# Six durations in a host-side scheduler of a decoder block set to the traced ones

## The chip, the cores and the metric

The kernel runs on one core of one Trainium2 chip. The metric is the device time of one launch in microseconds (us). The time before is the median of three runs.

The engines are named as the profile names them: PE (TensorE, with PEld for its weight loads), DVE (VectorE), ACT (ScalarE), POOL (GpSimd) and SP (the queue that issues the DMAs).

## What is computed

One decoder layer over 1024 tokens of width 1024: a normalisation modulated by a condition c, one wide projection, sparse attention and a Mamba-2 scan side by side, a gated merge, and a feed-forward part. Cut to what matters:

```python
h = rms_norm(x, norm1_w[l]) * (1.0 + sc1) + sh1
proj = h @ w_in[l]
q, kv, nsa_g, z, xbc, dt_raw, mg = jnp.split(proj, IN_OFFSETS, axis=-1)
...
o_attn = nsa_attention(q, kc, kv[:, :, 1], ks, kv[:, :, 3], kw, kv[:, :, 5], nsa_gates,
                       cmp_pe_k[l], cmp_w1_k[l], cmp_w2_k[l], cmp_pe_v[l], cmp_w1_v[l], cmp_w2_v[l])
...
xbc = jax.nn.silu(xbc)
...
y = ssd_chunked(xs, dt, a, bm, cm) + d_skip.astype(jnp.float32)[:, None] * xs.astype(jnp.float32)
y = y.reshape(b, s, SSM_INNER) * jax.nn.silu(z.astype(jnp.float32))
```

## The kernel before

**Tiling.** Every large product is float32, split into a high and a low part: `mm3k` (L319 to L324) issues three matmuls per k-tile, high times high, low times high and high times low (L322, L323, L324). Weights are loaded raw, ACT makes the high part `whi` (L351) and Pool the low part `wlo` (L353).

**Stages, in order of time.** The start (normalisation, `token_block` for keys, values and queries, up to about 250 us); the attention (two groups of heads g, eight query tiles i and two halves hq, units named g_i_hq), with the projections of x, z and m in its background; the scan (four groups g, eight chunks c, named g_c), with what is left of the background; the output projections and the second normalisation; the gated products (`gate_up`), from about 1860 us; `down` and the end.

**What sets the order.** A scheduler written in the host program, class `Flow`, decides in which order the instructions of each engine are written; the chip then runs each engine's queue in just that order. A stage is a set of generators that yield requests for PE: `yield (needs, cost, trace)`. `cost` is a number in us, and PE's own clock of the scheduler is advanced by it. Work of ACT, DVE, POOL and the DMAs is put into four queues with costs of its own, times `RESERVE` (1.15, 1.15, 1.2 and 1.0). The scheduler's clock picks what is ready first.

In the attention the background is a fill. It may go while its credit is above zero. The credit falls by the cost of each background request and grows by the cost of each main request times a fixed pace:

```python
            if s is fill:
                self.credit -= cost
            elif pace is not None:
                self.credit = min(self.credit + cost * pace(), 20.0)
```

**Names around the change.** In `background` (L1154 to L1281) blocks of kind x, z and m take turns. A block has four parts q, each with eight requests, accumulated into `fps`. For x, parts 0 and 2 are the first halves of the tokens; `finish_x` evacuates `fps` to `xr`, clears its first three columns on POOL (memset, L1173) if it is a first half, else copies them from the half before (L1179); then DVE makes three convolution steps into `u` (L1166), ACT a tanh, DVE a last step (L1184), and PE transposes u to `xsT` (L1199), which is stored to `xsd`.

A modulation row is made on POOL in `mod_rows` (L1377 to L1394): four loads of `w_ada`, each scaled (L1389), and eight sums into `acc` (L1392).

In the attention, `tp` is the transposed probability P (L2353), `kv` the copy of it in float32 halves (ACT L2356 the high one, DVE L2357 the low one), and `o` takes the value products (L1100). POOL scales P (L2287). `kv0` and `kv1` are also the tiles of keys and values of the two groups, loaded at L1057. DVE's and ACT's writes go to the two spare parts of the same tile.

In the scan, per chunk: `cb` (L2434), `bdm` (DVE L2436), the decay `E` (eight DVE instructions, L2422), the diagonal product `yd` (L2454) that reads `xs` (loaded at L2401), `yo` (L2463) and `sp` (L2485).

## Time and profile before

| | us |
|---|---|
| median of three runs | 2515.34 (2510.87 to 2517.52) |
| the profiled execution, its time | 2509.3 |
| its span | 2507.5 |
| PE busy | 2433.3 |
| DVE busy | 1784.3 |
| ACT busy | 1240.3 |
| POOL busy | 1163.9 |

The span runs from the first to the last instruction of the profiled execution; 1.8 us of its time lie around it. A wait is the idle time of an engine ahead of an instruction, put down to what released it last. The chain of work that ended last is for 81% PE.

### The profile page before, as it was taken

How to read it: one execution, taken by the hardware profiler on the slowest of the kernel's cores; microseconds unless marked ns; L12 is line 12 of the kernel's file. 1: busy time of each engine (PE TensorE's matmuls, PEld its weight loads, DVE VectorE, ACT ScalarE, POOL GpSimd, SP SyncE). 2: the span in 40 equal slices, each digit the busy share in tenths (PEclk: the TensorE clock that was granted, in tenths of full speed). 3: DMA queues.
4: the chain of work that ended last, by engine and by line, in shares of the span. 5: the costliest groups of instructions: out<-in, count | busy, mean ns of one | idle time of the engine just before them, and what ended most of it. 6: DMA issues, size and time to landing. Idle time of an engine off the chain costs nothing.

```text
span 2507.5 us, 39721 instructions
## 1 busy us (share of the span) xinstructions
PE 2433.3 (97%) x13674; PEld 2081.8 (83%) x13674; DVE 1784.3 (71%) x3917; ACT 1240.3 (49%) x2644; POOL 1163.9 (46%) x917
## 2 busy tenths in 40 slices
PE   5999999999999999999999999999999999999998
PEld 5999788899888988988777777878988888887886
DVE  7644788867766788776567886778767676765858
ACT  4422677666655676656456555532443323323543
POOL 2112474656464747455534342201245565655853
PEclk8999999999999999999999999999999999999999
DMA  7432443333335433235467876426343332326853
GB/s 252 132 126 83 158 120 96 89 102 110 93 102 167 141 97 114 81 104 187 145 192 233 266 228 193 147 76 225 137 173 101 105 106 93 113 92 233 308 169 118
DMA packets 274474, 363.91 MB, mean 145 GB/s; under 512 B 22232, under 2 KB 177624, under 8 KB 273760
## 3 DMA queue, kind: packets, MB, share of 16 engines
q1 hardware_dynamic: 274272, 361.37, 44.8%
q8 instruction: 108, 1.77, 0.3%
q14 instruction: 94, 0.77, 0.1%
HBM read 256.05 MB, written 105.25 MB: 144 GB/s over the span
## 4 chain that ended last, share of the span: by engine, by line
PE 81%; DVE 9%; DMA 4%; ACT 3%; issue 2%; POOL 1%; SPq 0%; DVEq 0%; ACTq 0%; POOLq 0%
PE fps L322 7%; PE fps L324 6%; PE fps L323 6%; PE gu L323 6%; PE gu L322 6%; PE gu L324 6%; PE o L1100 4%; PE S L2269 4%; PE tp L2353 4%; PE dps L324 2%; PE dps L323 2%; PE dps L322 2%; PE sps L322 2%; PE tokps L324 2%; PE tokps L322 2%; PE tokps L323 2%
## 5 line engine op out<-in xcount | busy, mean ns | idle before, releaser
L2287 POOL TENSOR_SCALAR P<-P,sm,gate 128x640 f32<-128x640 f32 (+7 forms) x256 | 228.0, 901 | 275.2 <-DVE sm L2284 176.1
L2357 DVE TENSOR_TENSOR kv<-tp,kv 128x512 fp32r<-128x512 f32 (+1 forms) x296 | 191.9, 657 | 103.1 <-ACT kv L2356 101.8
L2356 ACT ACTIVATE kv<-tp 128x512 fp32r<-128x512 f32 (+1 forms) x296 | 167.1, 574 | 183.7 <-PE tp L2353 174.9
L2278 ACT ACTIVATE P<-P,sm 128x640 f32<-128x640 f32 (+7 forms) x256 | 187.2, 733 | 50.4 <-DVE sm L2274 48.2
L1100 PE MATMUL o<-kv 128*128 128x512 f32 x528 | 189.2, 407 | 6.1 <-DVE kv L2357 3.5
L2269 PE MATMUL S<-kv,Q 128*128 128x384 f32 (+5 forms) x768 | 183.6, 336 | 5.1 <-DVE sm L2274 4.3
L322 PE MATMUL fps<-hT_hi,whi_x 128*128 128x512 f32 x384 | 160.4, 418 | 0.7 <-ACT xs L1209 0.7
L2274 DVE CUSTOM_DVE_ANT_0 P<-S,kb 128x256 f32<-128x256 f32 (+5 forms) x256 | 121.3, 493 | 49.2 <-PE tp L2353 31.9
L2353 PE MATMUL tp<-id,P 128*128 128x128 f32 x1056 | 155.2, 273 | 0.0
L324 PE MATMUL fps<-hT_hi,wlo_x 128*128 128x512 f32 x384 | 151.2, 394 | 0.0
L323 PE MATMUL fps<-hT_lo,whi_x 128*128 128x512 f32 x384 | 150.9, 393 | 0.0
L322 PE MATMUL fps<-whi_z,hT_hi 128*128 128x256 f32 x512 | 150.4, 294 | 0.0
L2269 PEld LDWEIGHTS S<-kv,Q 128*128 128x128 f32 x768 | 128.1, 189 | 25.5 <-DVE sm L2274 8.5
L1923 DVE TENSOR_TENSOR ex<-ex,gu 128x512 f32<-128x512 f32 x120 | 80.9, 684 | 94.5 <-PE gu L324 93.8
L1166 DVE SCALAR_TENSOR_TENSOR u<-xr,hcw,u 128x512 f32<-128x512 f32 x144 | 138.9, 967 | 10.9 <-ACT u L1169 7.3
L2353 PEld LDWEIGHTS tp<-id,P 128*128 128x128 f32 x1056 | 128.2, 140 | 22.1 <-issue 0.2
L324 PE MATMUL fps<-whi_z,hT_lo 128*128 128x256 f32 x512 | 144.8, 283 | 0.0
L323 PE MATMUL fps<-wlo_z,hT_hi 128*128 128x256 f32 x512 | 144.6, 282 | 0.0
L1758 ACT ACTIVATE x1r<-ex 128x512 fp32r<-128x512 f32 x102 | 62.9, 627 | 121.1 <-POOL ex L1776 60.4
L1100 PEld LDWEIGHTS o<-kv 128*128 128x128 f32 x528 | 96.0, 189 | 24.9 <-DVE kv L2357 8.0
L2427 POOL TENSOR_TENSOR dx<-xs,hd 128x512 f32<-128x512 f32 x32 | 41.8, 1308 | 160.0 <-DVE yy L2469 123.4
L322 PE MATMUL fps<-hT_hi,whi_m 128*128 128x512 f32 x256 | 113.7, 444 | 0.0
(480 smaller groups left out, 8042.1 us busy)
## 6 DMA issues: line engine op xcount, KB each, us to landing
wada<-w_ada SPq DMA_DIRECT2D x40, 512.0 KB, 4.3
actd<-ex SPq DMA_DIRECT2D x69, 256.0 KB, 2.0
ex<-actd SPq DMA_DIRECT2D x69, 256.0 KB, 4.0
ac<-acd SPq DMA_DIRECT2D x32, 512.0 KB, 4.7
raw_x<-w_in SPq DMA_DIRECT2D x24, 512.0 KB, 4.6
ws<-w_down SPq DMA_DIRECT2D x44, 256.0 KB, 3.6
wsd<-ws SPq DMA_DIRECT2D x88, 128.0 KB, 1.8
ff<-w_gate SPq DMA_DIRECT2D x22, 512.0 KB, 4.9
```

Source lines behind the costliest of these rows:

```text
L322: mm(ps, lh, rh, start=k == 0, stop=False)
L323: mm(ps, lh, rl, start=False, stop=False)
L324: mm(ps, ll, rh, start=False, stop=k == kt - 1)
L1100: nc.tensor.matmul(o.t.rearrange("p h q -> p (h q)"), vst(), pair()[m], start=n + m == 0, stop=n == u.total - 1 and m == 1)
L1166: return lambda: nc.vector.scalar_tensor_tensor(u.t, xr[:, k:k + N2], hcw[:, ft, k:k + 1], u.t, op0=OP.mult, op1=OP.add)
L2269: mm(sp[:, :w], q, kvb.kv[:, br, r, first + c0:first + c1], start=r == 0, stop=r == 1)
L2274: nc.vector.tensor_tensor_reduce(P[:, c0:c1], sp[:, :w], k.kb[:, m0:m0 + w], scale=-1.0, scalar=sm[:, 0, h:h + 1] if p else 3.0e38, op0=OP ...
L2278: ex = A(0.26 + 0.8333e-3 * n, [mx], lambda: nc.scalar.activation(P[:, :n], P[:, :n], AF.Exp, bias=sm[:, 1, h:h + 1], scale=-1.0, accum_ou ...
L2287: nc.gpsimd.tensor_scalar(P[:, :n], P[:, :n], sm[:, 3, m:m + 1], k.gate[:, i, self.h0 + m, br + 1:br + 2], op0=OP.mult, op1=OP.mult)
L2353: nc.tensor.transpose(tp[:, h * 128:h * 128 + 128], P, k.id)
L2356: hi = A(0.064 + 0.104 * n, [op, pair], lambda: nc.scalar.activation(pair()[0][:, c], tp[:, c], AF.Copy))
L2357: lo = V(0.068 + 0.133 * n, [hi], lambda: nc.vector.tensor_sub(pair()[1][:, c], tp[:, c], pair()[0][:, c]))
```

## The change

Six cost numbers of requests are other ones: of the token products (`tokps`), of the background products (0.72 for z, 0.69 for x and m, where both had 0.685), of the output projection (`ops`), of the sums of `turn_x` on POOL, of the gated products (`gu`) and of the down products (`dps`). No instruction is added or taken away.

```diff
--- before.py
+++ after.py
@@ -658,7 +658,7 @@
                 for k in range(8):
                     while self.hop[t0 // 2][k // 2] is None:
                         yield None
-                    op = yield ([W.ops[k], ps, self.hop[t0 // 2][k // 2]], 0.356, lambda t=t, k=k, s=s, ps=ps: self.mm3k(
+                    op = yield ([W.ops[k], ps, self.hop[t0 // 2][k // 2]], 0.363, lambda t=t, k=k, s=s, ps=ps: self.mm3k(
                         ps[:, t], k, 8, self.hT_hi[:, k, s], self.hT_lo[:, k, s], W.hi[:, k], W.lo[:, k]))
             if kd == "kv":
                 self.kv_evac(b, t0, ps, op)
@@ -1261,7 +1261,7 @@
                             c, s = slice(m * 128, (m + 1) * 128), slice(h * N2, (h + 1) * N2)
                             self.mm3k(ps.t, k, 8, W.hi[:, k, c], W.lo[:, k, c], self.hT_hi[:, k, s], self.hT_lo[:, k, s])
                         need = W.ops[k]
-                    op = yield ([need, ps], 0.685, mm)
+                    op = yield ([need, ps], 0.72 if kd == "z" else 0.69, mm)
                     if n > len(self.order) - 3 and k == 3:
                         while self.o[0] is None:
                             yield None
@@ -1617,7 +1617,7 @@
             ps = self.buf("s", [128, 256], "ops")
             for k in range(8):
                 m = lambda r, k=k: r[:, 2 * (t % 2) + k // 4, k % 4, 64 * (t - t % 2):64 * (t - t % 2) + 128]
-                op = yield ([W.ops[k], self.mop[t // 4][k], ps], 0.356, lambda: self.mm3k(
+                op = yield ([W.ops[k], self.mop[t // 4][k], ps], 0.359, lambda: self.mm3k(
                     ps.t, k, 8, m(self.M0), m(self.M1), W.hi[:, k], W.lo[:, k]))
             left[n] -= 1
             if left[n] == 0:
@@ -1702,7 +1702,7 @@
 
             def add(E, need, o, x, y, op=OP.subtract, cost=None):
                 eng = nc.vector if E is V else nc.gpsimd
-                return E(cost or (0.6 if E is V else 1.23), need, lambda: eng.tensor_tensor(o(), x(), y(), op=op), first=True)
+                return E(cost or (0.6 if E is V else 1.45), need, lambda: eng.tensor_tensor(o(), x(), y(), op=op), first=True)
 
             def copy(need, o, x, cost=0.52):
                 return A(cost, need, lambda: nc.scalar.activation(o(), x(), AF.Copy), first=True)
@@ -1904,7 +1904,7 @@
                     (hi, lo), (rh, rl) = (r[:, 128 * k:128 * k + 128] for r in pc.t), moving[p](k)
                     self.mm3k(ps.t, k, 4, hi, lo, rh, rl)
 
-                op = yield ([w, ps] + need, 0.685, product)
+                op = yield ([w, ps] + need, 0.697, product)
             pc.until(op)
             self.ff_sums(s, p, q, b, ps, op)
         self.ffend = op
@@ -2139,7 +2139,7 @@
                         outs.clear()
                 (xp, xe), (wp, we) = self.dl[p, b]
                 ps, js = banks[j], slice(128 * j, 128 * j + 128)
-                op = yield ([xe, we, ps], 0.685, lambda: self.mm3k(
+                op = yield ([xe, we, ps], 0.69, lambda: self.mm3k(
                     ps.t, b, NB, xp.t[0][:, js], xp.t[1][:, js], wp.t[0], wp.t[1]))
                 if j == 3:
                     xp.until(op)
```

Of PE's 11,800 rows the order is the same in the gated and down stages. From the attention's first unit to the scan's last group it is another one; a few rows of the start move too. Numbers at the ends of names are those of tiles; they differ between the programs.

**POOL, where group 0 of the attention ends and block x7 runs in the background.** `acc31` is a modulation row, `wlo_z4` the low part of the next block's weights, `xr` the tile whose head is cleared. Before, the row of the clearing for part 0 of x7 stands behind the first sum:

```order
L1389 TENSOR_TENSOR wada312_8136<-wada312_8136,sc_75 128x1024
L1392 TENSOR_TENSOR acc31_8171<-acc31_8171,wada310_8134 128x512
L1173 MEMSET xr_8223 128x3
L1392 TENSOR_TENSOR acc31_8171<-acc31_8171,wada310_8134 128x512
L1392 TENSOR_TENSOR acc31_8171<-acc31_8171,wada312_8136 128x512 x2
L1389 TENSOR_TENSOR wada314_8278<-wada314_8278,sc_75 128x1024
L2287 TENSOR_SCALAR P0_7_1_8194<-P0_7_1_8194,sm0_7_1_8067,gate_1659 128x640
```

After, it stands behind the last sum and the first half of wlo_z4:

```order
L1392 TENSOR_TENSOR acc31_8193<-acc31_8193,wada316_8298 128x512
L2287 TENSOR_SCALAR P0_7_1_8226<-P0_7_1_8226,sm0_7_1_8021,gate_1659 128x640
L1392 TENSOR_TENSOR acc31_8193<-acc31_8193,wada316_8298 128x512
L353 TENSOR_TENSOR wlo_z4_8426<-raw_z4_0_8375,whi_z4_8411 128x1024
L1173 MEMSET xr_8310 128x3
L353 TENSOR_TENSOR wlo_z4_8426<-raw_z4_4_8429,whi_z4_8411 128x1024
L1140 TENSOR_TENSOR ws51_8452<-ws51_8452 128x256 x3
L1173 MEMSET xr_8506 128x3
```

The second clearing (xr_8506), of part 2, which before stood ahead of the second half of wlo_z4, is now behind it and three rows of `ws51` (a repeated row is printed once, with its count).

**DVE, at the same place.** Before, the convolution of part 0 (u_8246 from xr_8223) runs between the exponentials of the last unit:

```order
L1166 SCALAR_TENSOR_TENSOR u_8246<-xr_8223,hcw_76,u_8246 128x512
L1113 TENSOR_TENSOR ot0_7_0_8269<-o0_7_0_7806,ob0_7_0_8253 64x256
L1114 TENSOR_TENSOR ot0_7_0_8269<-o0_7_0_7806,ob0_7_0_8253 64x256
L1166 SCALAR_TENSOR_TENSOR u_8246<-xr_8223,hcw_76,u_8246 128x512
L2274 ISA P0_7_1_8244,sm0_7_1_8067<-S0_7_1_8250,kb_85,sm0_7_1_8067 128x384
```

After, it is the u_8317 from xr_8310, with three of the unit's steps for `kv0` behind its first row:

```order
L2357 TENSOR_TENSOR kv0_2840<-tp0_7_1_8415,kv0_2840 128x512
L2357 TENSOR_TENSOR kv0_2840<-tp0_7_1_8421,kv0_2840 128x512
L1184 SCALAR_TENSOR_TENSOR u_8389<-xr_8385,u_8389 128x512
L1166 SCALAR_TENSOR_TENSOR u_8317<-xr_8310,hcw_76,u_8317 128x512
L2357 TENSOR_TENSOR kv0_2840<-tp0_7_1_8446,kv0_2840 128x512
L1166 SCALAR_TENSOR_TENSOR u_8317<-xr_8310,hcw_76,u_8317 128x512
L2357 TENSOR_TENSOR kv0_2840<-tp0_7_1_8460,kv0_2840 128x512
L1166 SCALAR_TENSOR_TENSOR u_8317<-xr_8310,hcw_76,u_8317 128x512
L2357 TENSOR_TENSOR kv0_2840<-tp0_7_1_8475,kv0_2840 128x512
L1184 SCALAR_TENSOR_TENSOR u_8317<-xr_8310,u_8317 128x512
```

The kv0 rows are those that the last value products of group 0 read; they were ahead of or between other blocks' steps, and three of them now come behind a step that reads what POOL has cleared.

**PE, at the start of the scan.** `yd0_0` to `yd0_5` are the diagonal products of chunks 0 to 5 of group 0. Before, those of chunks 0 and 1 have only sp and cb between them, and the load of xs for chunk 2 follows the use of its buffer by chunk 0:

```order
L323 MATMUL fps_14205<-hT_lo_214,whi_m4_13998 128x512
L324 MATMUL fps_14205<-hT_hi_210,wlo_m4_14002 128x512
L2454 MATMUL yd0_0_14245<-xs0_0_14129,E0_0_14153 128x64 x8
L2485 MATMUL sp0_0_14254<-xw0_0_14137,bdm0_0_14131 128x512
L2434 MATMUL cb0_2_14256<-bct0_2_14180 128x128
L2454 MATMUL yd0_1_14271<-xs0_1_14141,E0_1_14184 128x64 x8
L322 MATMUL fps_14205<-hT_hi_210,whi_m4_13998 128x512
```

After, yd0_1 is followed by its yo, and 78 background matmuls stand between yd0_1 and yd0_2 (24 before):

```order
L323 MATMUL fps_14145<-hT_lo_214,whi_m4_14036 128x512
L324 MATMUL fps_14145<-hT_hi_210,wlo_m4_14043 128x512
L2434 MATMUL cb0_2_14214<-bct0_2_14181 128x128
L2454 MATMUL yd0_1_14216<-xs0_1_14102,E0_1_14126 128x64 x8
L2463 MATMUL yo0_1_14227<-st0_0_14186,bct0_1_14098 128x512
L322 MATMUL fps_14145<-hT_hi_210,whi_m4_14036 128x512
L323 MATMUL fps_14145<-hT_lo_214,whi_m4_14036 128x512
```

Chunks 3 to 5 stand closer after. Before, yd0_3 had 27 background matmuls up to yd0_4:

```order
L322 MATMUL fps_14494<-hT_hi_210,whi_m5_14035 128x512
L323 MATMUL fps_14494<-hT_lo_214,whi_m5_14035 128x512
L324 MATMUL fps_14494<-hT_hi_210,wlo_m5_14046 128x512
L2454 MATMUL yd0_3_14500<-xs0_3_14348,E0_3_14371 128x64 x8
L322 MATMUL fps_14494<-hT_hi_210,whi_m5_14035 128x512
L323 MATMUL fps_14494<-hT_lo_214,whi_m5_14035 128x512
```

After, yo and sp follow yd0_3 at once, and 12 matmuls, of which the first two rows are shown, lead to yd0_4 (and again 12 from there to yd0_5):

```order
L323 MATMUL fps_14487<-hT_lo_214,whi_m5_14176 128x512
L324 MATMUL fps_14487<-hT_hi_210,wlo_m5_14190 128x512
L2434 MATMUL cb0_4_14508<-bct0_4_14462 128x128
L2454 MATMUL yd0_3_14510<-xs0_3_14377,E0_3_14350 128x64 x8
L2463 MATMUL yo0_3_14533<-st0_2_14478,bct0_3_14233 128x512
L2485 MATMUL sp0_3_14537<-xw0_3_14442,bdm0_3_14359 128x512
L322 MATMUL fps_14487<-hT_hi_210,whi_m5_14176 128x512
L323 MATMUL fps_14487<-hT_lo_214,whi_m5_14176 128x512
```

## Rows read from the trace of the kernel before

**Rows 1.** The page: busy time of PE, share of the span, instructions.

```profile
PE 2433.3 (97%) x13674; PEld 2081.8 (83%) x13674; DVE 1784.3 (71%) x3917; ACT 1240.3 (49%) x2644; POOL 1163.9 (46%) x917
```

**Rows 2.** Windows: busy us (instructions) of PE, PEld, DVE, ACT, POOL; PEclk; DMA; GB/s.

```profile
750.00:800.00 50.00, 46.57 (x331) 43.23 (x330) 27.22 (x81) 24.89 (x76) 22.58 (x28) 0.97 0.59 187
1250.00:1300.00 50.00, 47.77 (x229) 37.74 (x229) 27.08 (x67) 28.83 (x66) 19.45 (x13) 0.97 0.60 186
713.80:745.10 31.30, 31.30 (x171) 26.44 (x170) 22.27 (x48) 18.97 (x41) 25.41 (x18) 1.00 0.35 100
754.70:758.10 3.40, 3.40 (x17) 3.10 (x16) 3.08 (x4) 1.76 (x3) 2.08 (x1) 0.50 0.58 177
1302.00:1312.00 10.00, 10.00 (x52) 7.86 (x50) 9.20 (x26) 6.25 (x16) 3.68 (x4) 1.00 0.58 190
```

**Rows 3.** Waits of PE, whole span: total us, times, longest us.

```profile
PE h2T L1668 <- ACT x L1649: 3.7, 3, 2.7
PE xsT L1199 <- DVE u L1184: 2.1, 2, 1.8
PE gu L323 <- DVE M L1705: 1.9, 1, 1.9
PE yd L2454 <- DMA xs<-xsd: 1.7, 1, 1.7
PE fps L324 <- POOL wlo_m L353: 1.7, 1, 1.7
PE kT L746 <- DVE kk L714: 1.6, 1, 1.6
PE hidmm L960 <- DMA w1whi<-cmp_w_k: 0.9, 1, 0.9
```

**Rows 4.** Timeline of POOL near x7: start, us, line, operation, count, idle before.

```profile
713.80 3.76 POOL L1389 TENSOR_TENSOR wada<-wada,sc 128x1024 f32<-128x1024 f32 x2
717.50 1.29 POOL L1392 TENSOR_TENSOR acc<-acc,wada 128x512 f32<-128x512 f32 x1
718.73 0.10 POOL L1173 MEMSET xr<- 128x3 f32 x1
728.56 0.88 POOL L2287 TENSOR_SCALAR P<-P,sm,gate 128x640 f32<-128x640 f32 x1 [2.49 <-DVE sm L2284]
734.67 1.64 POOL L2287 TENSOR_SCALAR P<-P,sm,gate 128x640 f32<-128x640 f32 x1
736.27 1.73 POOL L1392 TENSOR_TENSOR acc<-acc,wada 128x512 f32<-128x512 f32 x1
742.73 2.41 POOL L353 TENSOR_TENSOR wlo_z<-raw_z,whi_z 128x1024 fp32r<-128x1024 f32 x1 [2.07 <-ACT whi_z L351]
```

**Rows 5.** Timeline of DVE, the held convolution step.

```profile
746.08 4.01 DVE L1166 SCALAR_TENSOR_TENSOR u<-xr,hcw,u 128x512 f32<-128x512 f32 x2 [2.70 <-POOL xr L1173]
```

**Rows 6.** Timeline of PE, z's products, transposes and a value product.

```profile
747.73 1.03 PE L2353 MATMUL tp<-id,P 128*128 128x128 f32 x8
748.52 0.37 PE L322 MATMUL fps<-whi_z,hT_hi 128*128 128x256 f32 x1
749.33 0.28 PE L322 MATMUL fps<-whi_z,hT_hi 128*128 128x256 f32 x1
750.05 0.40 PE L1100 MATMUL o<-kv 128*128 128x512 f32 x1
```

**Rows 7.** DMA queue SP, the load of kv1; the tile kv's landing time.

```profile
764.14 0.82 SPq L1057 DMA_DIRECT2D kv<-kvd  x2
...
DMA to landing us min/median/max: 7.1/7.1/7.1
```

**Rows 8.** Timeline of DVE, eight decay steps E of a chunk each.

```profile
1294.20 5.13 DVE L2422 SCALAR_TENSOR_TENSOR E<-E,dt,bdm 128x128 f32<-128x128 f32 x8
1303.64 2.97 DVE L2422 SCALAR_TENSOR_TENSOR E<-E,dt,bdm 128x128 f32<-128x128 f32 x8
1313.85 2.19 DVE L2422 SCALAR_TENSOR_TENSOR E<-E,dt,bdm 128x128 f32<-128x128 f32 x8
```

## The prediction, made before the change ran

> **What bounds the kernel now.** The page's table of engines comes first: PE is busy 2433.3 us of a span of 2507.5 [rows 1], so 74.2 us are waits, and no new order can win more than these plus what a lowered clock costs. The windows of 50 us say where in the stretches that the change moves: PE works 46.57 of 50 at 750 and 47.77 at 1250 [rows 2]. The waits of PE, by whom they wait for, then give the single prices [rows 3]: the long ones behind the start are single events, 1.8 us for u, 1.7 for xs, 1.7 for wlo_m, 2.7 for x, 1.9 for M. [...]
>
> The profiled execution took 2509.3 us, 6.0 below the median of 2515.34. I work out a difference on its rows and apply it to the median.
>
> **The change part by part.** Nothing is removed or added: the six numbers are only costs in the host's scheduler, and each engine has the same instructions as before. Busy time is therefore taken as unchanged, at 0. If neighbours change, DVE and Pool prices change too (below). What can change is who waits for whom.
>
> *Gated and down products, 0.697 and 0.69; turn_x's sums, 1.45.* PE's order of the gate and down products is the same before and after, and the order of DVE, ACT and Pool around the transposes is too. So the waits for x (2.7) and M (1.9) [rows 3] stay: 0. If a swapped buffer moved them, they could lose or gain their own length and 1.7 of clock, 8.0 together at the very most. I take 0, since the instructions around them stand as they did.
>
> *Tokens and start, 0.363.* The load of the compress weights moves ahead of two stores, and the product waiting for it (0.9) comes 12 PE rows earlier. The wait may go. The wait of kT for kk (1.6) [rows 3] may grow by a like amount. Between -0.9 and +0.9 I take -0.5, since the load's own queue is shorter.
>
> *z at 0.72, x and m at 0.69.* This is the part that moves things. Background work is charged more against the credit, so fewer background products stand ahead of each step of the attention: 42 fewer at the start of group 1, 282 fewer in its middle, 54 fewer in the state-space scan, none at its end. Three places have long waits now.
>
> Place one, the change from group 0 to group 1. Before, Pool clears the head of xr for the first half of block x7 at 718.73, between sums of acc31, but for the third quarter only after the low part of z4's weights (742.73, 2.41 us) [rows 4]. DVE idles 2.70 us at 746.08 until that second clearing [rows 5], and PE's 1.8 us for u follow. After, the first clearing also stands behind the whole chain of acc31 and behind wlo_z4, and the held step on DVE has three additions to kv0 and the u of the transpose behind it. Counted from x7's first product, about where the chain starts, it is four scalings at 1.88, eight sums, four steps of P and one wlo at 2.41 [rows 4]. With sums at 1.29 and P at 0.88 this is 23.8 us, with 1.73 and 1.64 it is 30.3. From the first scaling to the end of wlo Pool worked 25.4 us before [rows 2], so I take that. PE reaches the transposes of that u after 72 products of 512 columns and 30 value products at an estimated 0.23 or, four of them, 0.12 (z's 256 columns take 0.12), and 54 transposes at 0.10 [rows 6]: 16.6 + 6.3 + 5.4, about 28.3 us. The u is ready some 5.3 us after the clearing, an estimate from its seven steps: three of the convolution and two additions between them at 0.7 to 0.75, the tanh and a last step. So PE waits 23.8 + 5.3 - 28.3 = 0.8 us at the fast end, 7.3 at the slow end and 2.4 between. With the clock these cost 0.8, 9.0 and 4.1, against the 1.8 + 1.7 = 3.5 that are paid now. The term is -2.7 to +5.5; I take +0.6, from the chain's work as it stood before.
>
> Of the same sum of acc31 there are rows of 1.29 and of 1.73 us [rows 4]. [...]
>
> At the same place kv1 replaces kv0. Its load, issued at 764.14 behind kv0's last value product, lands 7.1 us later [rows 7]; PE now has about 8.1 us of products between that product and the first score, where it had some 12. That just holds: +0.2, bounds 0 and +2.7 (a wait of 1 us and a clock drop).
>
> Place two, the last attention unit and block m4. The wait for wlo_m (1.7) [rows 3] comes from a weight load that stands behind two loads of w_ada on SP. It still does. m4 now comes about 5 us sooner on PE, while one of its loads stands one store earlier. I take 0, with bounds of -3.4 (it goes, with its clock) and +3.
>
> Place three, the start of the scan. The wait for xs (1.7) [rows 3] is that of chunk 2. Between the diagonal products of chunks 1 and 2 PE had 24 background products and 4.4 us of others, 9.9 us. Now there are 78 of them, 22 us. The load then is long there: -1.7 and -1.7 of clock, so -3.4. In return chunks 3, 4 and 5 stand closer: 12 products instead of 27 between yd0_3 and yd0_4, and 12 again up to yd0_5, 6.3 us each. From chunk 4's cb to yd0_5, PE has 12.6 us. DVE must do two decays E and the rest of one chunk in it. E cost 2.19 to 5.13 us for its eight, and the chunk between 1302 and 1312 used 9.20 us of DVE, 2.97 of it E [rows 2, 8]. So it needs 6.2 + 2 x 2.2 = 10.6 to 6.2 + 2 x 5.1 = 16.5. At 2.97 it needs 12.2 and just fits: 0, upper bound 3.9 and 1.7 of clock, 5.6.
>
> Sum: gated 0, start -0.5, handover +0.6, kv1 +0.2, m4 0, xs -3.4, chunks 0: -3.1. 2515.3 - 3.1 = 2512.2, said as 2512. The bounds of the terms without the gated stage add up to -0.9 - 2.7 - 3.4 - 3.4 = -10.4 and 0.9 + 5.5 + 2.7 + 3 - 3.4 + 5.6 = +14.3. I don't expect all on one side.
>
> **The rivals.** *Slower: DVE and Pool beside each other.* The order packs their work at places one and three, and every price there goes to its slow row. The handover gives +5.5 in place of +0.6, the chunks +5.6 in place of 0, kv1 +2.7 in place of 0.2: -3.1 + 4.9 + 5.6 + 2.5 = +9.9, so 2525.2. It decides from the point where the sums of acc31 at the handover average over 1.5 us and the eight steps of E of chunks 4 and 5 take over 3 us. For it: 1.73 and 5.13 are rows of this trace. Against: the next E took 2.97, and DVE's convolution steps are held just while the chain runs. [...]
>
> *Faster: the three background waits all go.* With fewer background products ahead, and prices nearer the traced ones (six z products, from 749.33 to 750.05, take 0.72 us [rows 6], the new number), u, xs and wlo_m come in time. 1.8 + 1.7 + 1.7 and three clock drops of 1.7 are 10.3, plus 0.9 for the start: 11.2, so 2504. For it: each is a single event with a release that is late by under 2 us. Against: place one's clearing is behind more Pool work than before, not less.
>
> *The change reaches nothing.* The scheduler multiplies the other engines' costs by 1.15 to 1.2, so corrections of 1 to 5% lie inside its reserve, and one set of waits of a few us is replaced by another of the same size: 2515. This and the forecast lie in the same band.
>
> **How the numbers follow.** About 0.3%, 7.5 us, is what a measurement of this kernel can tell from no change. The forecast and the case that reaches nothing have 0.27 and 0.18, together 0.45 within 0.3%. The faster case has 0.30, as three waits that are late by so little are easily undone by a shift of a few us. The slower one has 0.25. The range takes in the three: 2501 (the faster case and 3 us under it, for short waits that go with it) to 2527 (the slower one and 2 over). Inside, the forecast's own range is 2507 to 2520.
>
> **What would show it.** Right: PE busy within 3 us of 2433; no wait of yd for xs over 1 us near the scan's start, and window 1250:1300 above 49; waits for x and M unchanged; at the handover DVE idle for Pool's clearing of xr, with a PE wait for u or kv of 1 to 4 us. Wrong: a wait of over 3 us for kv or u there, or of yd or yo for DVE in chunks 3 to 6; a row of new waits in group 1, whose mixture of attention and background changes most; new drops of the granted clock where there are none now; or the waits for x and M gone, which the order gives no reason for.

## The result and the profile after

The changed kernel took 2530.79 us (median of 5 runs, 2524.24 to 2535.08), the kernel before 2511.60 (2510.10 to 2517.52) in the same session. The ratio as compared is 1.0054 with the interval 1.0038 to 1.0070; the two medians alone stand 0.76% apart. It is slower, and the time lies above the forecast's range of 2501 to 2527. The profiled execution is the one of 2530.79, with a span 21.5 us longer than that of before.

The page's head says where not to look: PE is busy only 3.6 us more than in [rows 1], DVE 9.5 us more.

```profile
span 2529.0 us, 39714 instructions
PE 2436.9 (96%) x13674; PEld 2086.4 (83%) x13674; DVE 1793.8 (71%) x3917; ACT 1242.1 (49%) x2644; POOL 1161.8 (46%) x917
```

Next come windows by stage: from the start to the attention's first score, to the scan's first cb, to its last yd, to the last transpose of h2, to the end. Columns: interval, its length, busy us (instructions) of PE, PEld, DVE, ACT and POOL, granted clock, DMA share, GB/s. The fourth stage, 191.3 and 191.4 us long, is left out. The kernel before:

```profile
0.00:265.90 265.90, 235.35 (x1780) 223.67 (x1781) 156.75 (x564) 87.22 (x165) 47.65 (x32) 0.96 0.48 158
265.90:1266.80 1000.90, 983.94 (x5999) 861.11 (x5998) 731.89 (x1736) 630.28 (x1458) 572.59 (x522) 1.00 0.38 117
1266.80:1666.70 399.90, 391.15 (x1940) 311.16 (x1939) 306.49 (x795) 216.79 (x487) 127.45 (x95) 1.00 0.64 202
...
1858.00:2507.50 649.50, 635.26 (x2735) 515.13 (x2733) 443.62 (x513) 230.73 (x413) 381.71 (x248) 0.99 0.42 141
```

The changed kernel, then two windows of the prediction, one of the scan's chunks, and two of the stretches at the lower clock:

```profile
0.00:263.30 263.30, 232.66 (x1767) 221.70 (x1768) 153.45 (x562) 85.25 (x162) 47.26 (x31) 0.96 0.49 159
263.30:1265.50 1002.20, 974.92 (x5957) 856.41 (x5956) 740.32 (x1738) 629.75 (x1453) 562.70 (x519) 0.99 0.37 114
1265.50:1690.70 425.20, 408.44 (x1995) 323.63 (x1994) 312.06 (x795) 221.82 (x495) 136.61 (x99) 0.98 0.61 197
...
1882.10:2529.00 646.90, 632.88 (x2735) 513.20 (x2734) 444.23 (x512) 230.22 (x413) 381.55 (x248) 0.99 0.43 142
...
750.00:800.00 50.00, 43.42 (x283) 38.50 (x282) 33.10 (x91) 28.91 (x85) 22.41 (x30) 0.93 0.52 169
1250.00:1300.00 50.00, 46.97 (x227) 37.04 (x226) 18.60 (x37) 24.30 (x47) 20.80 (x13) 1.00 0.57 181
1308.00:1350.00 42.00, 39.24 (x184) 29.20 (x182) 38.32 (x97) 24.03 (x57) 20.29 (x16) 0.96 0.66 209
...
609.10:612.50 3.40, 3.40 (x16) 3.13 (x15) 1.64 (x4) 1.20 (x2) 3.01 (x2) 0.50 0.00 0
783.20:786.60 3.40, 3.40 (x16) 3.40 (x17) 1.07 (x3) 0.38 (x1) 3.40 (x8) 0.50 0.61 183
```

The scan is 25.3 us longer (425.2 against 399.9). Of this 12.4 us is moved work: 54 background matmuls at 0.230 us (the mean step from one to the next in this trace, where no wait and no lowered clock lies between) that stood in the attention now stand in the scan. The start's 2.6 us are moved work too: nine background matmuls and four transposes that stood ahead of the first score now stand behind it, so PE's busy time there falls by 2.7 us and its idle time stays at 30.6. Counted with its own work, the attention lost 1.3 + 12.4 - 2.6 = 11.1 us and the scan 25.3 - 12.4 = 12.9; the start gained nothing and the last stage 2.6. Together 21.4 of the 21.5 us.

The two losses are waits and the clock that falls behind them. Length less PE busy is 27.3 us in the attention where it was 17.0, and 16.8 in the scan where it was 8.7. Between the start and the end the trace now has nine stretches of 3.4 us at granted clock 0.50, where it had five; eight of the nine lie in the attention and the scan, against three. At an estimated 1.7 us a stretch (half of its length; by the 0.427 us from one product of 512 columns to the next in it, against 0.230 outside, it would be 1.6) this makes 10.3 + 3.4 = 13.7 us in the attention and 8.1 + 5.1 = 13.2 in the scan. In the attention that is 2.6 more than was lost: PE was busy that much less there on the same work, which is not explained. The waits of PE name the places (waited for; us in total, times, longest us):

```profile
...
PE o L1100 <- DVE kv L2357: 11.4, 8, 3.1
PE fps L322 <- ACT xs L1209: 4.0, 3, 2.6
PE tp L2353 <- DVE Pc L2313: 3.6, 2, 2.4
PE h2T L1668 <- ACT x L1649: 3.4, 2, 2.7
PE aps L322 <- DVE rq L293: 3.2, 1, 3.2
...
PE yo L2463 <- DVE rq L294: 2.8, 1, 2.8
...
PE yo L2463 <- DVE st L2493: 2.6, 1, 2.6
PE yd L2454 <- DVE st L2493: 2.5, 1, 2.5
PE cb L2434 <- DMA bct<-bct: 2.3, 2, 1.9
...
PE kT L746 <- DVE kk L714: 1.6, 1, 1.6
...
PE gu L323 <- DVE M L1705: 0.9, 1, 0.9
PE xsT L1199 <- DVE u L1184: 0.8, 1, 0.8
```

Against [rows 3]: the single waits for xs from the DMA and for wlo_m (1.7 each) are gone, that for u fell from 1.8 to 0.8, and in their place stands a row of waits for DVE of 2.4 to 3.2 us; the longest for kv was 0.7 us before, for st 0.9. One view of how they arise, the timeline of the changed kernel (start, length, engine, line, operation, count, [idle before and its releaser]), around 608, at the handover and in the scan:

```profile
601.76 2.47 DVE L1166 SCALAR_TENSOR_TENSOR u<-xr,hcw,u 128x512 f32<-128x512 f32 x1
601.79 4.20 POOL L1389 TENSOR_TENSOR wada<-wada,sc 128x1024 f32<-128x1024 f32 x2
604.16 2.11 DVE L2313 TENSOR_TENSOR Pc<-Pc,st 128x256 f32<-128x256 f32 x1
605.95 4.92 POOL L1392 TENSOR_TENSOR acc<-acc,wada 128x512 f32<-128x512 f32 x3
606.19 1.75 DVE L1166 SCALAR_TENSOR_TENSOR u<-xr,hcw,u 128x512 f32<-128x512 f32 x1
607.86 1.27 DVE L2357 TENSOR_TENSOR kv<-tp,kv 128x512 fp32r<-128x512 f32 x2
608.59 0.79 PE L1100 MATMUL o<-kv 128*128 128x512 f32 x2 [3.13 <-DVE kv L2357]
...
748.62 2.73 POOL L353 TENSOR_TENSOR wlo_z<-raw_z,whi_z 128x1024 fp32r<-128x1024 f32 x1 [2.34 <-ACT whi_z L351]
751.29 0.10 POOL L1173 MEMSET xr<- 128x3 f32 x1
...
759.54 0.50 PE L1100 MATMUL o<-kv 128*128 128x512 f32 x1 [1.54 <-DVE kv L2357]
760.88 0.66 PE L1199 MATMUL xsT<-id,u 128*128 128x128 f32 x4 [0.84 <-DVE u L1184]
...
778.71 1.05 ACT L351 ACTIVATE whi_x<-raw_x 128x1024 fp32r<-128x1024 f32 x1
...
782.53 0.57 ACT L1209 ACTIVATE xs<-xsT 128x512 f32<-128x512 f32 x1
783.15 0.56 PE L322 MATMUL fps<-whi_z,hT_hi 128*128 128x256 f32 x1 [2.61 <-ACT xs L1209]
...
1312.46 2.05 PE L2463 MATMUL yo<-st,bct 128*128 128x512 f32 x2 [2.76 <-DVE rq L294]
1435.58 0.77 PE L322 MATMUL aps<-o,whi_ao 128*128 128x512 f32 x1 [3.21 <-DVE rq L293]
```

Ahead of 608 three DVE steps in a row meet Pool's chain for a modulation row: 2.47, 2.11 and 1.75 us for steps that take 0.75, 0.41 and 0.75 when no Pool instruction runs. The copy that PE needs stands behind them, and PE waits 3.13 us. The same happens at 333 (2.44 for Pc), 496 (1.88 for kv) and 873 (2.54 for kv).

### The profile page after: what moved, and what is told of

Its sections match the earlier page's. It is cut to its first block, busy times and chain, and to the rows that moved or that the text cites. A ratio compares the mean times of both kernels' runs of the same rounds, so it can differ in the third digit from the quotient of the medians.

```text
span 2529.0 us, 39714 instructions
## 1 busy us (share of the span) xinstructions
PE 2436.9 (96%) x13674; PEld 2086.4 (83%) x13674; DVE 1793.8 (71%) x3917; ACT 1242.1 (49%) x2644; POOL 1161.8 (46%) x917
## 4 chain that ended last, share of the span: by engine, by line
PE 56%; DVE 6%; ACT 2%; DMA 1%; issue 1%; POOL 0%; SPq 0%; DVEq 0%; ACTq 0%; POOLq 0%
PE gu L323 6%; PE gu L322 6%; PE gu L324 6%; PE fps L322 3%; PE fps L324 3%; PE fps L323 3%; PE dps L324 2%; PE dps L323 2%; PE dps L322 2%; PE sps L322 2%; PE sps L324 2%; PE sps L323 2%; PE o L1100 2%; PE tp L2353 2%; PE S L2269 2%; PE yd L2454 2%
## 5 line engine op out<-in xcount | busy, mean ns | idle before, releaser
L2287 POOL TENSOR_SCALAR P<-P,sm,gate 128x640 f32<-128x640 f32 (+7 forms) x256 | 221.0, 874 | 275.0 <-DVE sm L2284 231.9
L2357 DVE TENSOR_TENSOR kv<-tp,kv 128x512 fp32r<-128x512 f32 (+1 forms) x296 | 191.9, 658 | 105.6 <-ACT kv L2356 104.1
L1100 PE MATMUL o<-kv 128*128 128x512 f32 x528 | 188.4, 405 | 12.2 <-DVE kv L2357 11.4
L1166 DVE SCALAR_TENSOR_TENSOR u<-xr,hcw,u 128x512 f32<-128x512 f32 x144 | 148.3, 1033 | 12.0 <-ACT u L1169 9.5
L2427 POOL TENSOR_TENSOR dx<-xs,hd 128x512 f32<-128x512 f32 x32 | 43.3, 1353 | 175.2 <-DVE yy L2469 130.9
```

Source lines behind the costliest of these rows:

```text
L1100: nc.tensor.matmul(o.t.rearrange("p h q -> p (h q)"), vst(), pair()[m], start=n + m == 0, stop=n == u.total - 1 and m == 1)
L1166: return lambda: nc.vector.scalar_tensor_tensor(u.t, xr[:, k:k + N2], hcw[:, ft, k:k + 1], u.t, op0=OP.mult, op1=OP.add)
L2287: nc.gpsimd.tensor_scalar(P[:, :n], P[:, :n], sm[:, 3, m:m + 1], k.gate[:, i, self.h0 + m, br + 1:br + 2], op0=OP.mult, op1=OP.mult)
L2357: lo = V(0.068 + 0.133 * n, [hi], lambda: nc.vector.tensor_sub(pair()[1][:, c], tp[:, c], pair()[0][:, c]))
```

## The experiments

Each time is a median, with the ratio to the kernel before in the same session and its 95% interval. Three theories run through them. **Credit:** the new numbers take income from the background, which lags behind. **Draw:** any small change deals a new order, and the waits of an order are partly luck; the order before lies at the good end. **Holds:** the waits come from DVE steps that a running Pool instruction holds; the expectations call this "Pool" or "collisions", and the draw "scatter". A fourth, "prices", has it that the new numbers give PE's clock of the scheduler too little lead.

### One part of the table at a time

```diff
- op = yield ([need, ps], 0.685, mm)
+ op = yield ([need, ps], 0.72 if kd == "z" else 0.685, mm)   e3_z
+ op = yield ([need, ps], 0.685 if kd == "z" else 0.69, mm)   e7_xm
- op = yield ([W.ops[k], ps, self.hop[t0 // 2][k // 2]], 0.356, ...
+ op = yield ([W.ops[k], ps, self.hop[t0 // 2][k // 2]], 0.363, ...   e8_tok
```

> The kernel before with z's products at 0.72 alone. Theory 'prices': z's correction is by far the largest (5%), so it carries most of the loss, +10 to +20 us. Theory 'credit': z is 8 of 28 blocks, 8 x 8 x 4 x 0.035 = 9 us of credit of about 12 that the change takes, so +8 to +15. Theory 'scatter': a draw of its own, -2 to +20.

Measured: 2515.9, 1.0028 [1.0012, 1.0044].

> The kernel before with x's and m's products at 0.69 alone (0.7%). Theory 'credit': 20 of 28 blocks at 0.16 us each take 3.2 us of credit, 4 or 5 requests, so +2 to +5 us. Theory 'scatter': a draw of its own, 0 to +15, with waits where DVE's stretched steps happen to stand ahead of something PE needs.

Measured: 2525.4, 1.0052 [1.0032, 1.0072].

> The kernel before with the token products at 0.363 alone. The start of the changed kernel was 2.6 us shorter (first score at 263.3 instead of 265.9). If that is this number's doing, the first score comes at 263 to 264 here too. What the moved credit does later is open: theory 'scatter' gives -3 to +12 us in all, theory 'credit' -3 to -1, since no background cost is changed.

Measured: 2515.5, 1.0018 [1.0002, 1.0034]; the first score comes at 265.3 us, not at the 263 to 264 expected. What follows: each of these three parts alone costs something, and what it costs has no relation to its size: 0.7% on x and m costs 0.52%, 5% on z 0.28%. Nor does the token number alone make the start 2.6 us shorter. By "prices" z alone should have cost 10 to 20 us; it cost 5.5. The other three numbers were not run alone.

### A change of 0.15%, and the credit by itself

```diff
- op = yield ([need, ps], 0.685, mm)
+ op = yield ([need, ps], 0.686, mm)   e1_eps
+ op = yield ([need, ps], 0.684, mm)   e14_epsm
- pace = (5.48 * 4 * (len(self.order) - 2) + 30) / total
+ pace = (5.37 * 4 * (len(self.order) - 2) + 30) / total    e2_low_pace
+ pace = (5.594 * 4 * (len(self.order) - 2) + 30) / total   e13_high_pace; e4_all_pace (on the changed kernel)
```

> The kernel before with one number changed by 0.15%: all background products (z, x, m) cost 0.686 where they had 0.685. Theory 'scatter' (any small change of the table deals a new order with a handful of other waits, and the order of before happens to be a good one): +8 to +20 us over the kernel before, as with the change, though nothing in the table has become truer or less true. Theory 'credit' (dearer background is let in less, so attention and scan stand barer): 0.15% of the credit is 0.9 us of some 600, one or two requests, so 0 to +2 us. Theory 'prices' (the new numbers themselves give PE's clock too little lead of DVE): 0 to +1 us.

Measured: 2512.8, 1.0011 [1.0000, 1.0022].

> The kernel before with all background products at 0.684 (0.15% less). Theory 'credit' and theory 'prices': -2 to +1 us. Theory 'scatter': 0 to +15 us.

Measured: 2525.5, 1.0044 [1.0028, 1.0060].

> The kernel before with the income of the background credit cut by 2% (5.48 to 5.37 in the pace of the attention), no cost changed. It lets in the same 17 or 18 requests fewer by the end of the attention as the change did (54 matmuls). Theory 'credit': +12 to +20 us, the whole loss of the change. Theory 'prices': 0 to +2 us, since PE's clock is as before. Theory 'scatter': anything from 0 to +20, most likely +8 to +18, with waits at other places than in the changed kernel.

Measured: 2527.6, 1.0065 [1.0047, 1.0082].

> The kernel before with the income of the background credit raised by 2% (5.48 to 5.594), no cost changed: the mirror of the run with the lower income, which lost some 16 us. Theory 'credit' (less background beside the attention is what costs): -3 to +2 us. Theory 'scatter' (any new order is a draw, and that of before lies at the good end of the draws): +2 to +15 us, with waits of PE of 1.5 to 5 us behind held DVE steps at new places.

Measured: 2513.7, 1.0001 [0.9986, 1.0016].

> The changed kernel, all six numbers, with the income of the credit raised by as much as the background has become dearer (5.48 to 5.594 in the pace of the attention), so that as many background requests are let in by the attention's end as before. Theory 'credit': the loss goes, 0 to +4 us over the kernel before. Theory 'prices': it stays, +12 to +20. Theory 'scatter': a draw of its own, most likely +5 to +20, with waits at other places than in the changed kernel.

Measured: 2519.7, 1.0042 [1.0027, 1.0057]. What follows: the run with 2% less income looks like the credit's effect, and taken alone would have been told as the cause, though it left only 24 more background matmuls to the scan and not the expected 54. But 0.684 gives the background more room (6 fewer are left) and still costs 0.44%, the mirrored run with 2% more income (36 fewer) gives nothing, and giving the changed kernel its income back (3 more) leaves 0.42%. Nor do the single parts fit: z alone leaves 36 more and costs 0.28%, x and m 12 more and 0.52%. The credit as the only cause falls. The eight neighbouring orders, these five and the three above, lie from 0 to 0.65% above the one before and none below. That is what the draw expects of an order at the good end, though two of its own forecasts missed: +8 to +20 us for 0.686 and +2 to +15 for the higher income both came out within 3 us of the kernel before.

### The long background stretch in the scan

The first guess about the scan was its 78 background matmuls in a row ahead of chunk 2, behind which chunks 3 to 6 crowd. The cause of the 78: dx of chunk 0 (Pool, L2427) takes the one buffer `acc` that the transposes of the last modulation row release, and these wait in the background until block m5. The edit issues that row one block earlier.

```diff
-            if n % 3 == 1 and sums:
+            if (n % 3 == 1 or n == 24) and sums:
```

> The changed kernel with one step moved: the last modulation row is summed on PE (adar, L1402) at the start of background block 24 (m4) instead of block 25 (m5). Its tile acc is the only buffer c7, which the scan's first dx (L2427) waits for. Theory 'adar' (the dearer background is some 54 matmuls behind when the scan starts, so adar comes later, dx of chunk 0 and the load of xs for chunk 2 with it, 78 background matmuls are let through in one lump, and chunks 3 to 7 then come faster than DVE can follow): the lump shrinks from 78 to 15, the waits of PE for DVE at 1312, 1355, 1396 and 1436 us mostly go, and the stretch from the first cb to the last yd falls from 425 to 408 to 416 us, the whole by 8 to 16. Theory 'Pool' (these waits are DVE steps held by Pool): the stretch stays within 4 us of 425.

Measured: 2527.7, 1.0052 [1.0034, 1.0069]. The stretch fell from 78 to 15, and the waits at 1312, 1355 and 1396 went. But one of 5.0 us came at 1429 and one of 2.3 at 1504, and the scan kept its length (424.5 us). So the long stretch caused those three waits, but without it others took their place, and it alone is not the loss.

> The kernel before with the same move of adar. There the lump is 24 matmuls and becomes 33 in the written order, and the scan had one wait for xs at 1289. Theory 'adar': little to gain, -4 to +2 us (the wait for xs and its clock may go). Theory 'Pool': 0 to +2 us.

Measured: 2515.9, 0.9995 [0.9985, 1.0005]. The order before had no such stretch to lose.

### Pool's long instructions cut

Scalings and low parts of 1024 columns are issued as four of 256, sums of 512 as two. The scheduler's costs, and so the order, stay as they are.

```diff
...
-            x = G(2.3, [d], lambda k=k, raw=raw: nc.gpsimd.tensor_tensor(
-                raw.t, raw.t, self.sc[:, k:k + 2, None].to_broadcast([128, 2, 512]), op=OP.mult))
+            x = G(2.3, [d], lambda k=k, raw=raw: [nc.gpsimd.tensor_tensor(raw[:, m, c:c + 256], raw[:, m, c:c + 256],
+                self.sc[:, k + m, None].to_broadcast([128, 256]), op=OP.mult) for m in range(2) for c in (0, 256)])
...
-                e = G(1.23, [x, e], lambda m=m, raw=raw: nc.gpsimd.tensor_tensor(acc.t, acc.t, raw[:, m], op=OP.add))
+                e = G(1.23, [x, e], lambda m=m, raw=raw: [nc.gpsimd.tensor_tensor(acc[:, c:c + 256], acc[:, c:c + 256], raw[:, m, c:c + 256], op=OP.add) for c in (0, 256)])
```

> The kernel before, its order on every engine unchanged, with Pool's instructions of 1024 columns (the low parts of weights L353, the scaling L1389) written as four of 256 and its sums L1392 of 512 as two of 256. Theory 'collisions' (a DVE step with two SBUF inputs that meets a running Pool instruction is held until that instruction ends, so a long Pool instruction costs such a step up to 2.4 us): the longest L1166 falls from over 2 us to about 1.4, DVE's excess in the attention from 100 us to 50 to 70, and the time by 3 to 10 us, since few of this order's waits stand behind a collision. Theory 'bandwidth' (both engines are merely slower while they run together): DVE's excess is unchanged within 10%, Pool's work grows by some 0.1 us for each added instruction, and the time is 0 to +5 us.

Measured, on the order before: 2499.3, 0.9952 [0.9933, 0.9971].

> The changed kernel with the same split of Pool's long instructions, its order unchanged. In the changed kernel 9 of the 13 waits of PE over 1.2 us in the attention and the scan stand behind 3 to 6 us by which DVE's steps were stretched in the 8 us ahead. Theory 'collisions': the waits at 333, 496, 609, 873, 1355, 1396 and 1436 us shrink by more than half, and the time falls by 12 to 25 us, to within 8 us of the kernel before or under it. Theory 'bandwidth', and theory 'order alone' (DVE has too much work between two needs of PE in the new order, whatever Pool does): it stays within 4 us of the changed kernel, +15 to +22 over the kernel before.

Measured, on the changed order: 2515.6, 1.0022 [1.0004, 1.0040]. Engines of the first, and Pool's groups by shape (count; busy us, mean ns):

```profile
PE 2426.9 (97%) x13674; PEld 2080.0 (83%) x13674; DVE 1754.3 (70%) x3917; ACT 1237.5 (50%) x2644; POOL 1234.4 (49%) x1311
```

```profile
L1392 POOL TENSOR_TENSOR acc<-acc,wada 128x256 f32<-128x256 f32 x128 | 96.0, 777 | 0.0
L1389 POOL TENSOR_TENSOR wada<-wada,sc 128x256 f32<-128x256 f32 x128 | 80.2, 662 | 12.2 <-DMA wada<-w_ada 12.1
```

Pool works 70.5 us more than in the profile before, yet DVE works 30.0 us less with the same instructions, and the time falls by 11.1 us. The attention takes 988.1 us in place of 1000.9, without a stretch at the lower clock where there were two. Its DVE steps run 73 us over their usual lengths in place of 100 (usual is the length below which a fifth of the steps of one line and shape lie), and 3 of them, scan included, are over by more than 1.5 us in place of 19. The longest L1166 took 2.27 us in place of 2.97, not the 1.4 expected.

In the changed order the attention takes 993.3 in place of 1002.2, in an execution 7 us slower than the median of this version. The waits at 333, 496, 609, 759 and 873 are gone (no wait over 0.9 us is left there), and PE's waits for kv fall from 11.4 to 0.9 us in all. The scan's four, from 1312 to 1436, stay at 2.1 to 2.6 us, against the expectation that they would halve. One line of the page and two of the waits show both:

```profile
L1100 PE MATMUL o<-kv 128*128 128x512 f32 x528 | 187.1, 403 | 1.1 <-DVE kv L2357 0.9
...
PE yd L2454 <- DVE st L2493: 2.6, 1, 2.6
PE yo L2463 <- DVE rq L294: 2.4, 1, 2.4
```

So the holds have a price, in both orders, and they made those five waits of the attention. But the two orders still differ by 16 us: long holds alone do not make the changed order the worse one. The split version of the changed order also has waits of its own, at 460 and 484, of 4.6 and 4.5 us. The first, in its timeline:

```profile
453.71 0.17 DVE L2309 RECIPROCAL st<-st 128x4 f32<-128x4 f32 x1
453.72 4.63 POOL L1389 TENSOR_TENSOR wada<-wada,sc 128x256 f32<-128x256 f32 x8
453.92 5.80 DVE L2310 TENSOR_TENSOR st<-st,gate 128x4 f32<-128x4 f32 x1
458.29 1.43 POOL L1392 TENSOR_TENSOR acc<-acc,wada 128x256 f32<-128x256 f32 x2
459.65 0.54 DVE L2274 CUSTOM_DVE_ANT_0 P<-S,kb,sm 128x320 f32<-128x320 f32 x1
460.25 0.56 PE L2269 MATMUL S<-kv,Q 128*128 128x320 f32 x2 [4.58 <-DVE sm L2274]
```

A step on 4 columns, 0.16 us at its shortest, takes 5.80: it waits through eight Pool pieces and the two sums behind them, which follow each other without a gap.

### The two together, and a gap between the pieces

> The kernel before with both edits. If their effects add: 2499 us of the split alone, less 0 to 4, so 2495 to 2500. Theory 'scatter' (each new order is a draw): 2495 to 2512.

Measured: 2496.4 (2495.5 to 2497.4), 0.9928 [0.9912, 0.9945]. This is faster than both kernels and the lowest time of the study, though its interval overlaps that of the split alone.

> The changed kernel with adar moved and with Pool's long instructions split in pieces of 256 columns. If the two losses are separate (the attention's by Pool holding DVE, the scan's by adar), their gains add: 15 us of the split and 8 to 16 of adar, so 2500 to 2508 us, at or under the kernel before. If they are one, it is no better than either alone, 2514 to 2520.

Measured: 2509.9, 0.9976 [0.9963, 0.9990]: the same pair on the changed order, 13.5 us behind. The attention takes 988.6 us and the scan 417.0, where the split alone had 425.8: with Pool's instructions cut, the move of the modulation row shortens the scan by 8.8 us, which it did not do by itself.

The last two try to let DVE in between the pieces, with a one-column Pool memset behind each. Of two theories, 'handover' has it that a DVE step gets in at such a memset, 'queue' that it does not:

```diff
-  [nc.gpsimd.tensor_tensor(...) for ...]
+  [(nc.gpsimd.tensor_tensor(...), nc.gpsimd.memset(self.spc, 0.0)) for ...]
```

> The changed kernel with Pool's long instructions split in pieces of 256 columns and, behind each piece, a Pool memset of one column to a scratch tile. With the split alone a DVE step of 128x4 was held 5.80 us across eight pieces in a row, so the pieces hand the hold on to each other. [...] Theory 'queue' (Pool's next piece is already asked for when the memset runs): excess as with the split alone, the time 0 to +4 us over it.

Measured, on the split changed order: 2509.3, 0.9980 [0.9963, 0.9997]. It stands 0.4% below the split alone, across two sessions. But the memset is not shown to be what lets DVE in: the excess in the attention is 78 us against 80 with the split alone, where 'handover' needed a clear fall. One step of 4 columns still took 7.11 us. It passed three memsets, then seven Pool instructions that have none; the first rows:

```profile
1133.18 7.11 DVE L2310 TENSOR_TENSOR st<-st,gate 128x4 f32<-128x4 f32 x1
1133.35 0.10 POOL L353 MEMSET spc<- 128x1 f32 x1
1133.40 0.74 POOL L353 TENSOR_TENSOR wlo_m<-raw_m,whi_m 128x256 fp32r<-128x256 f32 x1
...
1140.21 0.68 DVE L2357 TENSOR_TENSOR kv<-tp,kv 128x512 fp32r<-128x512 f32 x1
```

> The best kernel so far (before, adar moved, Pool's long instructions split; 2496 us) with the same one-column memsets. Theory 'handover': 2488 to 2494. Theory 'queue': 2496 to 2500.

Measured: 2499.5, 0.9937 [0.9914, 0.9959]: nothing gained over the version without memsets.

## Why the prediction was wrong

**Where it failed.** The failing step is the list of terms itself. The text named three places that "have long waits now" and summed only what would become of them; busy time was "taken as unchanged" and the rest of the attention stood at 0. The order between 266 and 1690 us was dealt anew throughout, and the attention's loss came from places without a wait before: at 333, 496, 609 and 873 the waits are 2.4 + 1.9 + 3.1 + 2.5 = 9.9 us, and two of them lowered the clock, 1.7 each. These 13.3 us had no term, and cutting Pool's instructions in the same order removes all four waits. With the handover below they come to more than the 11.1 us of the attention, since the wait for wlo_m and its clock and short waits went. The sentence on new waits in group 1 stood under what would show it wrong, and only the wait at 873 lies in group 1; new waits should have been a term. The 1.7 us of clock in the terms is half of the 3.4 us at granted clock 0.50 in [rows 2], behind the wait for u; no run shows that every long wait brings such a stretch, and behind the waits of 2.4 at 333 and 2.5 at 873 the granted clock stayed at 1.00. The other step that failed is a size: the crowding of the scan's chunks, taken at 0.

**Point by point.**
- *Gated and down, 0:* the wait for x stayed at 2.7, as said; that for M fell from 1.9 to 0.9, against it, and the stretch at the lower clock that followed it, at 1864 before, is gone. Together 1.0 + 1.7 = 2.7, about what the last stage gained, where 0 was taken.
- *Start, -0.5:* the wait for the compress weights went, that of kT stayed at 1.6. The start is 2.6 us shorter, but by work that moved behind the first score and not by waits: its idle time is the same. That the sign fits is luck, and the reason given is not shown. The token number alone moves the same nine matmuls and gives 265.3 us.
- *Handover, +0.6:* PE's wait for u came out at 0.8, the fast end, but by luck. From x7's first product (727.55) the clearing took 23.8 us, as the fast end had it, only because Pool's chain had begun 4.5 us earlier; from its first scaling it took 28.3, with 4.2 us of waits, 2.3 of them for ACT's whi_z. Then u was there 9.5 us after the clearing and not 5.3, since DVE came to it 2.2 us late and two of its steps were held (2.09 and 1.24 us). PE came after 32.5 us and not 28.3, so two misses of 4.2 cancel. The sums did run at their fast length here, all eight between 1283 and 1296 ns, and DVE did not idle for the clearing, though that had been named as a sign of being right. Of the 64 such sums in the changed kernel's trace, 12 took over 1.48 us, up to 1.75.
- *Beside the handover's term:* kv came 1.5 us late, u 0.8 and an evacuation of xs by ACT 2.6 us, because exponentials and a weight's high part were queued ahead of it. The clock fell twice. From 757 to 787 these cost 1.5 + 0.8 + 0.7 + 0.7 + 2.6 + 2 x 1.7 = 9.7 us where 3.5 were paid, so +6.2. The window 750:800 shows it: PE works 43.42 of 50, against 46.57 [rows 2]. ACT stood in no term.
- *kv1, +0.2:* no wait there; held.
- *Place two, 0:* the wait for wlo_m fell from 1.7 to 0.4 and lowers the clock no more, inside the bounds.
- *xs, -3.4:* right, the wait is gone. But window 1250:1300 has 46.97, not over 49: the cb of the scan's second chunk stands in that window and now waits 1.9 us for its load (bct).
- *Chunks, 0 with an upper bound of 5.6:* too small. Between 1303 and 1440 there are waits of 2.8, 2.5, 2.6 and 3.2 us and four clock drops, 11.1 + 6.8 = 17.9 us. In the window 1308:1350 DVE is busy 38.32 of 42 us, so a step that comes late is hardly caught up: the crowding was foreseen for two chunks and went on for more. The mechanism was the one named, its size was not. Less the 3.4 of xs and some short waits this is the 12.9 of the scan.

**The rivals.** The slower one had the right mechanism, DVE and Pool beside each other, but two places and a chance of 0.25. By its own test it would have been rejected: the sums averaged 1.29, not over 1.5. The contention of the two was priced only on Pool's side (do its sums take 1.29 or 1.73 us?) and not on DVE's (how many held steps in a row stand ahead of one that PE needs?).

**What is settled and what isn't.** Shown: the time went mostly into waits of PE for DVE (and one for ACT) and the clock behind them. The attention's new waits for DVE are steps held by Pool, since in the same order they go when Pool's instructions are cut, and the cut takes 13 us from the attention in one order and 9 in the other. Three of the scan's four stand behind the stretch of 78, since they go with it. Counted in the traces, DVE's steps in the attention ran 100 us over their usual lengths before and 102 after (77 and 85 if the median is taken as usual), so the sum changed little; the number of steps that were over by more than 1.5 us, scan included, rose from 19 to 27. Of 13 waits over 1.2 us after, 11 have 3 to 5.3 us of such excess in the 8 us ahead of them, against 2 of 6 before; of all stretches of 8 us, 4% before and 6% after have as much. Rejected: the credit as the one cause, and the stretch of 78 as the one cause of the scan's loss. Supported, not proved: that the order before was a lucky one. Its eight neighbours in cost are all equal or slower. Open: why the changed order stays 13.5 us behind with both edits in both, and why a given order groups its held steps ahead of PE's needs.

## What to carry to other kernels

When a change re-deals a whole list-scheduled order, the waits of the old trace are no inventory of the new one's: give the waits that don't exist yet a term, sized by how often a step PE needs stands behind two or three that Pool can hold. Judge a table of costs by several neighbouring tables, since here 0.15% of one number moved the time by 0.1 and 0.4%; truer numbers gave no better order in a scheduler that has no notion of the conflict that sets many of the waits. Cut long Pool instructions that run beside a busy VectorE, even if Pool then works 6% more: here it was worth 0.5%.

## What the chip showed that I had not expected

- A DVE step with two SBUF inputs, or one of the copies of 3 columns, that is lengthened ends some 10 to 30 ns (up to 4 columns), 0.15 us (128 columns), 0.28 (256) or 0.55 (512) behind the end of a Pool instruction. Of the steps over by more than 0.3 us in the attention and scan, 125 before and 134 after, all but one began while a Pool instruction ran. Of the 296 copies of P at L2357, which read one input from PSUM, some 175 began beside a running Pool instruction in each trace, and none took over 0.69 us.
- The size of a held step sets that last piece and not how long it is held: 128x4 took 5.80 us in the split changed order and 7.11 with the memsets, 128x3 (the copy at L1175) 5.95 in the former.
- The hold may outlast the instruction that began it. With Pool's pieces back to back, the step of 5.80 us waited through ten of them; let in after the first it would have taken under 0.7 us, an estimate from the 4.63 us of the first eight. Cutting shortens most holds, not all.
- PE's granted clock fell to 0.50 behind single waits of 1.9 to 3.1 us at 496, 609 and 783, for 3.4 us each time, as it had at 1.8 before [rows 2]; but the waits of 2.4 at 333 and 2.5 at 873 left it at 1.00.
